# In-projection of a two-layer diffusion step: more unused products at the start, adaLN units turned one chunk sooner, the last quarter's weights in the load list

## The chip, the core and the metric

The kernel runs on one core of a Trainium2 chip. The core has a matrix engine (TensorE, PE, whose loads of the stationary operand are listed apart as PEld), VectorE (DVE), ScalarE (ACT), GpSimd (POOL), and SyncE (SP), which here issues every DMA. Each engine executes its own instructions in the order in which the program holds them and waits on semaphores for the others. The metric is the device time of one launch, in microseconds; the median of three runs before the change is 2295.28 us.

## What is computed

One inference step of a transformer with two layers, on 128 context tokens and 128 latent tokens. Both groups use the same weights; the latent tokens also attend to cached keys. Only the first sub-layer matters for this case:

```python
mod = silu(cond) @ w_ada[l] + b_ada[l]                 # shift, scale, gate of each sub-layer
sh1, sc1, gt1, sh2, sc2, gt2 = split(mod, 6)
h = rmsnorm(x, g_norm_mix[l]) * (1 + sc1) + sh1        # (256 tokens, 2048)
proj = h @ w_in                                        # 2048 -> 768 + 512 + 64 + 1024 + 256 + 256
q_lat, ckv, k_rope, qb, kb, vb = split(proj)
qa  = rmsnorm(q_lat, g_q) @ w_q_up
ckv = rmsnorm(ckv, g_kv)                               # latents of this call
ckv_all = concat([cached_ckv, ckv])                    # cached latents ahead of them
kv = ckv_all @ w_kv_up
kb = rope(rmsnorm(kb, g_kn))
```

Everything is float32. A product of two float32 matrices is made of three products of a format with fewer bits: each operand is split into a high part (a cast) and a low part (what the cast left over), and high x high, high x low and low x high are added up.

## The kernel before

**Layout.** Features lie on the 128 partitions, the 256 tokens of both groups side by side in the free dimension. `hx` holds the modulated rows: 16 tiles of 128 features, each with a high half and a low half. `w_in_ab` comes as blocks of 128 x 128; an output chunk of 128 features needs 16 of them.

**Stages of the in-projection.** The rows need adaLN scales and shifts that are themselves products with 2 MB to 4 MB of weights, so the projection doesn't wait for all of them. It goes over 23 output chunks several times, each time with a part of the 16 feature tiles, and adds to the result in SBUF: `part(whole, 0, 2, ...)` uses feature tiles 0 and 1, `part(halves, 2, 2, ...)` tiles 2 and 3, and `part(rest, 4 * q, 4, ...)` for q = 1, 2 and 3 four tiles each. The text calls the last three quarters 1, 2 and 3; quarter 3 is the last quarter. In a quarter a chunk is four blocks, three products each, so 12 products.

**AdaLN units.** A unit is 512 columns of the adaLN weights. Between chunks, `pair` multiplies the condition with two tiles of such weights (PE, tile `ada`), ACT copies the result (`am`), PE transposes it (L113), DVE reduces it and adds the bias (L455, L457), and the rows of the next quarter can be made from it (`rows`, that is `modulate`): per row two scalings, one on DVE (L688) and one on ACT (L691), a cast on ACT (L692) and a subtraction (L674). The table in `quarter(q)` says after which chunk each step comes. In quarters 1 and 2 the transposes and rows came after chunk 16, and `normed` (DVE) after chunk 12.

**Weights.** `feed` is a list written out by hand: tiles of adaLN weights and tiles of `w_in_ab` (16 blocks, 1 MB, tile `raw`, three buffers) in the order in which SP loads them, each as soon as a buffer of its kind is free. `lead(W, n)` runs before each chunk while a loaded tile of the list is left: it casts 8 blocks (two casts of four blocks on ACT, `wh`, L258, and two subtractions on DVE, `wl`, L259, both in `split`) until 12 blocks are ready. These casts are pinned in program order by `keep_order`. A tile that isn't in the list is loaded and cast inside `chunk()`, 8 blocks at a time, and a scheduler puts these where it thinks best. Before the change the list had 13 of the 18 tiles of `rest`; the last five, all of the last quarter, were outside.

**Beside the last quarter.** `finish(c)` starts the norms and ropes of queries, latents and keys as their chunks arrive. `deep` runs sums of further adaLN rows on DVE (L538, a custom op, two per loaded `block`), pinned, and `row_step` those on PE. `caches()` loads the cached latents (`ckc`) and keys and splits `ckc` into `kv_in`.

**The start.** PE first runs `WARM` products on zeros (L110, `acc<-am`), then the two first half units: sums of the scale unit, statistics of x, `spread` (the norm's factor over the partitions), transposes, sums of the shift unit, transposes, and then the first products with weights.

```python
def lead(W, n):
    while len(W.blocks) < n and (W.half or W.begun):
        W.ahead(keep_order)
```

Of the kernel before, what the change touches and what calls it, by code (L numbers as in the profile page):

```python
# [18 lines left out]
P = 128  # L19
D = 2048  # L20
KD = D // P
T = 128
# [27 lines left out]
    _n += _w  # L50
NCONST = _n
NEARLY = _AT["bada"][0] + 2 * KD
WARM = 9
RATE = {"in0": 0.35, "in": 0.5, "in3": 0.25, "heads": 0.72, "out0": 0.62, "c": 0.36, "outc": 0.36}
FRATE = {"up": 0.7, "down": 1.42}
PEW = {"heads": 1.0, "out0": 1.0, "c": 1.0}
# [38 lines left out]
def step_kernel(ctx: ExitStack, tc: tile.TileContext, A: dict):  # L95
# [24 lines left out]
    pe = TensorE()  # L120
# [44 lines left out]
    x = T_(keep, [P, KD, NT], "x")  # L165
# [69 lines left out]
    def acc_bank(n=None):  # L235
        if n is None:
            n = accs[turn["acc"] % len(accs)]
            turn["acc"] += 1
        return T_(pacc, [P, 512], f"acc{n}")
# [17 lines left out]
    def split(out_hi, out_lo, src, pin=lambda i: i):  # L257
        pin(act.copy(out_hi, src))  # L258
        pin(dve.tensor_tensor(out=out_lo, in0=src, in1=out_hi.bitcast(F32), op=ALU.subtract))  # L259
# [693 lines left out]
    def mixer_ab(hx, beside):  # L953
        l = 0
        with tc.tile_pool(name="ab", bufs=1) as ab:
            with tc.tile_pool(name="abp", bufs=1) as pj:
                T_(ab, [P, SHIFT // 4], "pad")
                spare = {"s3": T_(ab, [P, 4, 512], "kv_in")}
                ckc = T_(pj, [P, 4, T], "ckc")
# [3 lines left out]

                def caches():
                    keep_order(sp.dma_start(out=ckc, in_=A["cache_ckv"]))
                    split(kv_in[:, :, 0, T:2 * T], kv_in[:, :, 1, T:2 * T], ckc)
                    keep_order(sp.dma_start(out=kr[:, T:2 * T], in_=A["cache_krope"]))
                    keep_order(sp.dma_start(out=kg[:, :, T:2 * T], in_=A["cache_gqa_k"]))
                    keep_order(sp.dma_start(out=vg[:, 1], in_=A["cache_gqa_v"]))
# [35 lines left out]
                def half_sums(unit):  # L1005
                    pair_sums(("half", unit.j, unit.h), unit.sums)
# [6 lines left out]
                rest = Weights(A["w_in_ab"][6:], 4, 4, cycle=23)  # L1013
# [3 lines left out]
                def weights(w, parts=1):  # L1017
                    feed.add("raw", lambda: w.begin(parts))
# [20 lines left out]
                for q in (1, 2):  # L1039
                    for u, t in ((2 * q + 2, 0), (2 * q + 2, 2), (2 * q + 3, 0), (2 * q + 3, 2)):  # L1040
                        weights(rest)
                        units(u, t)
                        if (q, u, t) == (1, 4, 2):
                            feed.add("late", late_constants)
                    weights(rest)
                    weights(rest)
                feed.go()

                pe.in_turn = True
# [9 lines left out]
                for g in range(2):  # L1059
                    for i in range(4):  # L1060
                        pe.matmul(ps[:, g:g + 1], squared[:, i, g * T:(g + 1) * T], inv(D),
                                  start=(i == 0), stop=(i == 3))
# [7 lines left out]
                nts = scaled_rows(rb0, 0, 2)  # L1070
                unit = HalfUnit(0, 0, att_bank, att_bank)
                half_sums(unit)

                def first_rows():
                    unit.copy()
                    unit.turn()
                    for c in range(2):
                        begin_row(hx, nts[c], c)

# [71 lines left out]
                    yield  # L1151

                def finish(c):
                    if c == 7:
                        deep.silu()
                        deep.rate = SIDE["in3"]
                    if c < 6:
                        start(queries(c))
                    elif c < 10:
                        start(latents(c - 6))  # L1160
                    elif c == 10:
                        start(key_rope())
                    elif c < 13:
                        start(keys(c - 11))
                    elif c == 14:
                        start(values(0))
                    elif c == 15:
                        start(values(1))
# [22 lines left out]
                def normed(q):  # L1191
                    second["nt"] = []
                    for c in range(4 * q, 4 * q + 4):
                        h = T_(tmp, [P, NT], "nt", bufs=4)
                        keep_order(dve.tensor_tensor(out=h, in0=x[:, c], in1=rb0, op=ALU.mult))
                        second["nt"].append(h)
# [20 lines left out]
                def pair(u, t):  # L1217
                    unit_pair(ROWS[u], t)
                    if t == 2:
                        second["finish"] = ada_finish(*ROWS[u])  # L1220
                        second["finish"].pop(0)()

                def turned(q=0):
                    second["finish"].pop(0)()
                    if q:
                        rows(q)
# [14 lines left out]
                def quarter(q):  # L1241
                    u = 2 * q + 2
                    return {3: lambda: pair(u, 0), 6: lambda: pair(u, 2), 8: turned, 11: lambda: pair(u + 1, 0),
                            12: lambda: normed(q + 1), 14: lambda: pair(u + 1, 2), 16: lambda: turned(q + 1)}

                def at(steps):
                    return lambda c: steps[c]() if c in steps else None
# [7 lines left out]
                kv_in = T_(ab, [P, 4, 2, 3 * T], "kv_in", F32R)  # L1255
# [392 lines left out]
    with banks("pab") as ppool["ada"]:  # L1648
# [3 lines left out]
        ps = acc_bank()  # L1652
        for _ in range(WARM):
            keep_order(pe.matmul(ps, idle[:, :P], idle, start=True, stop=True))
# [5 lines left out]
        with tc.tile_pool(name="beside", bufs=1) as beside:  # L1660
            o = mixer_ab(hx, beside)
            with tc.tile_pool(name="raw", bufs=1) as rp:
                T_(rp, [P, SHIFT // 4], "pad")
                u = raw_tile(rp, "u")
# [5 lines left out]
    u = ffn(hx, W, *begun, 0, st)  # L1670
    stage[0] = "c"
    with tc.tile_pool(name="cc", bufs=1) as cp, banks("pc") as ppool["ada"]:
# [8 lines left out]
        u = mixer_c(cp, hx, W, begun[0], st)  # L1681
# [155 lines left out]
```

## Time and profile before

| | us |
|---|---|
| median of 3 runs (2294.23 to 2295.8) | 2295.28 |
| the profiled execution | 2295.23 |
| its span, first to last instruction | 2293.4 |
| PE busy | 2272.2 |
| DVE busy | 1880.7 |
| ACT busy | 1215.1 |
| mean granted clock of PE | 0.996 |

The profiled execution is 1.83 us longer than its span. How the lines are read: a row of the timeline has its start and length in us, the engine, the source line, the operation, the tile written and the tiles read, shapes and a count; in square brackets stands how long the engine was idle before it and what ended that. A row of a stretch has its bounds, then PE, PEld, DVE, ACT and POOL busy with their instruction counts, the granted clock of PE as a share of full speed, the share of the DMA engines and GB/s. A row of a group has busy time and mean length in ns, then idle time before the group. Products run into each other, so lengths overlap; distances of starts don't.

### The profile page before, as it was taken

To read this page: it belongs to the slowest core of one execution; us is meant where nothing else is said; L and a number is where in the kernel's file an instruction comes from. 1 tells how busy PE (TensorE), PEld (TensorE's weight loads), DVE (VectorE), ACT (ScalarE), POOL (GpSimd) and SP (SyncE) were. 2 spreads that over 40 slices of the span, in tenths; PEclk is the share of its full clock that TensorE was granted. 3 is DMA by queue.
4 is the path that set the end of the run, shared out by engine and by line. 5 is a ranking of instruction groups with operands and counts; after the bars stand their busy time and mean duration, and the time that the engine had idled before them with its cause. 6 is when DMAs were issued, how large, how long until landed. Compare 5 with 4: busy or idle time off the path is not lost.

```text
span 2293.4 us, 47509 instructions
## 1 busy us (share of the span) xinstructions
PE 2272.2 (99%) x19496; PEld 2180.4 (95%) x19496; DVE 1880.7 (82%) x2963; ACT 1215.1 (53%) x2049; POOL 190.9 (8%) x219
## 2 busy tenths in 40 slices
PE   9999999999999999999999999999999999999998
PEld 6788888999999999999999999999999999999998
DVE  4768878889989999999978988898899955666654
ACT  4446666765553355555575454557555434555543
POOL 0011104400000000001130000023000000000011
PEclk9999999999999999999999999999999999999999
DMA  9888988777778777777778888776677655555553
GB/s 394 363 354 307 333 329 349 288 264 255 260 259 296 293 274 258 257 268 257 286 292 301 324 316 308 264 273 224 255 260 258 256 201 196 191 198 189 200 188 127
DMA packets 100121, 617.14 MB, mean 269 GB/s; under 512 B 10752, under 2 KB 18880, under 8 KB 33344
## 3 DMA queue, kind: packets, MB, share of 16 engines
q1 hardware_dynamic: 99904, 614.11, 72.4%
q8 instruction: 153, 2.51, 0.4%
q14 instruction: 64, 0.52, 0.1%
HBM read 609.32 MB, written 4.75 MB: 268 GB/s over the span
## 4 chain that ended last, share of the span: by engine, by line
PE 96%; DVE 1%; DMA 1%; ACT 1%; POOL 1%; issue 0%; SPq 0%; DVEq 0%; ACTq 0%
PE acc L110 89%; PE ada L110 3%; PE att L110 2%; DMA raw<-w_in_ab 1%; PE misc L110 0%; DVE wl L259 0%; DMA araw<-w_ada 0%; PE att L113 0%; POOL dev L837 0%; PE ada L113 0%; PE misc L113 0%; ACT wh L258 0%; DVE x L1694 0%; POOL hxc L841 0%; DVE qb L1184 0%
## 5 line engine op out<-in xcount | busy, mean ns | idle before, releaser
L110 PE MATMUL acc<-hx,wh 128*128 128x256 f32 (+1 forms) x7232 | 1248.5, 278 | 3.7 <-ACT wh L258 1.5
L258 ACT CAST wh<-raw 128x1024 fp32r<-128x1024 f32 (+1 forms) x866 | 798.6, 938 | 825.5 <-PE acc L110 697.2
L259 DVE TENSOR_TENSOR wl<-raw,wh 128x1024 fp32r<-128x1024 f32 (+1 forms) x866 | 930.3, 1091 | 245.6 <-ACT wh L258 237.9
L110 PEld LDWEIGHTS acc<-hx,wh 128*128 128x128 f32 x7232 | 1092.8, 188 | 24.7 <-issue 14.2
L110 PE MATMUL acc<-hx,wl 128*128 128x256 f32 (+1 forms) x3616 | 1001.5, 277 | 0.8 <-DVE wl L259 0.7
L110 PEld LDWEIGHTS acc<-hx,wl 128*128 128x128 f32 x3616 | 680.0, 188 | 4.3 <-issue 1.7
L110 PE MATMUL acc<-g,wh 128*128 128x256 f32 x2816 | 478.8, 276 | 0.0
L110 PEld LDWEIGHTS acc<-g,wh 128*128 128x128 f32 x2816 | 423.9, 188 | 0.0
L110 PE MATMUL acc<-g,wl 128*128 128x256 f32 x1408 | 388.0, 276 | 0.0
L483 DVE CUSTOM_DVE_ANT_0 junk<-araw,condb 128x2048 f32<-128x2048 f32 x128 | 294.1, 2297 | 0.0
L110 PEld LDWEIGHTS acc<-g,wl 128*128 128x128 f32 x1408 | 264.2, 188 | 0.0
L211 POOL TENSOR_TENSOR sqacc<-sqacc,sq 128x256 f32<-128x256 f32 x62 | 72.2, 1165 | 1442.3 <-ACT sq L207 1437.6
L110 PE MATMUL acc<-hxc,wh 128*128 128x256 f32 (+1 forms) x1056 | 189.1, 281 | 0.0
L110 PEld LDWEIGHTS acc<-hxc,wh 128*128 128x128 f32 x1056 | 161.9, 188 | 1.8 <-issue 1.7
L110 PE MATMUL acc<-hxc,wl 128*128 128x256 f32 (+1 forms) x528 | 146.8, 278 | 0.0
L110 PEld LDWEIGHTS acc<-hxc,wl 128*128 128x128 f32 x528 | 99.5, 188 | 0.2
L110 PE MATMUL acc<-wh,hxc 128*128 128x256 f32 (+1 forms) x512 | 95.0, 283 | 0.8 <-DVE nt L848 0.8
L1587 ACT ACTIVATE cv<-acc,convw 128x256 f32<-128x256 f32 x169 | 94.4, 559 | 0.0
L538 DVE CUSTOM_DVE_ANT_0 hx<-block,condb 128x1024 fp32r<-128x1024 f32 x66 | 80.4, 1218 | 4.7 <-DMA block<-w_ada 4.4
L1593 DVE SCALAR_TENSOR_TENSOR cv<-acc,convw,cv 128x254 f32<-128x254 f32 x169 | 80.8, 478 | 3.2
L110 PEld LDWEIGHTS acc<-wh,hxc 128*128 128x128 f32 x512 | 79.4, 188 | 3.7 <-issue 2.5
L1590 DVE SCALAR_TENSOR_TENSOR cv<-acc,convw,cv 128x254 f32<-128x254 f32 x169 | 80.2, 474 | 0.0
(290 smaller groups left out, 1809.3 us busy)
## 6 DMA issues: line engine op xcount, KB each, us to landing
raw<-w_up SPq DMA_DIRECT2D x176, 1024.0 KB, 4.8
araw<-w_ada SPq DMA_DIRECT2D x132, 1024.0 KB, 6.2
raw<-w_down SPq DMA_DIRECT2D x88, 1024.0 KB, 4.8
raw<-w_in_c SPq DMA_DIRECT2D x48, 1024.0 KB, 6.9
block<-w_ada SPq DMA_DIRECT2D x42, 512.0 KB, 6.5
raw<-w_in_ab SPq DMA_DIRECT2D x18, 1024.0 KB, 9.0
raw<-w_out_ab SPq DMA_DIRECT2D x16, 1024.0 KB, 7.8
raw<-w_out_c SPq DMA_DIRECT2D x16, 1024.0 KB, 5.6
```

What stands on the lines that cost most here:

```text
L110: return self.placed(nc.tensor.matmul(*a, **kw))
L211: eng.tensor_tensor(out=st["acc"], in0=st["acc"], in1=sq, op=ALU.add)
L258: pin(act.copy(out_hi, src))
L259: pin(dve.tensor_tensor(out=out_lo, in0=src, in1=out_hi.bitcast(F32), op=ALU.subtract))
L483: keep_order(dve.tensor_tensor_reduce(out=T_(feat["pool"], [P, D], "junk"), in1=feat["row"][:, c], in0=feat["raw"].rearrange("p g n -> p ( ...
L538: keep_order(dve.tensor_tensor_reduce(out=self.junk, in0=self.raw, in1=self.row[:, c].rearrange("p (g n) -> p g n", g=2), scale=1.0, scala ...
L1587: pin(act.activation(y, ps, AF.Identity, scale=cw[:, 1, m:m + 1], bias=cw[:, 3, m:m + 1]))
L1590: pin(dve.scalar_tensor_tensor(out=y3[:, :, 1:], in0=p3[:, :, :T - 1], scalar=cw[:, 0, m:m + 1], in1=y3[:, :, 1:], op0=ALU.mult, op1=ALU.add))
L1593: pin(dve.scalar_tensor_tensor(out=y3[:, :, :T - 1], in0=p3[:, :, 1:], scalar=cw[:, 2, m:m + 1], in1=y3[:, :, :T - 1], op0=ALU.mult, op1=A ...
```

## The change

Five edits, all in the in-projection. `WARM` goes from 9 to 15. Four unused products (512 columns of x, into a bank that is overwritten later) are added: two behind the sums of the shift's half unit, two behind its transposes. In quarters 1 and 2 the second unit is turned, and the next quarter's rows are made, after chunk 15 and not after chunk 16. The split of the cached latents goes from `caches()` to chunk 3 of the last quarter. The five last tiles of `rest` are put into the list, so `lead` casts them as well.

```diff
-WARM = 9
+WARM = 15
...
                 def caches():
                     keep_order(sp.dma_start(out=ckc, in_=A["cache_ckv"]))
-                    split(kv_in[:, :, 0, T:2 * T], kv_in[:, :, 1, T:2 * T], ckc)
...
                     weights(rest)
+                    weights(rest)
+                for _ in range(5):
                     weights(rest)
                 feed.go()
...
                 half_sums(unit)
+                unused = acc_bank()
+
+                def idle_products(n):
+                    for _ in range(n):
+                        pe.matmul(unused, x[:, 0, :P], x[:, 0:2].rearrange("p c n -> p (c n)"), start=True, stop=True)
+
+                idle_products(2)
 
                 def first_rows():
                     unit.copy()
                     unit.turn()
+                    idle_products(2)
...
                 def finish(c):
+                    if c == 3:
+                        split(kv_in[:, :, 0, T:2 * T], kv_in[:, :, 1, T:2 * T], ckc)
...
-                            12: lambda: normed(q + 1), 14: lambda: pair(u + 1, 2), 16: lambda: turned(q + 1)}
+                            12: lambda: normed(q + 1), 14: lambda: pair(u + 1, 2), 15: lambda: turned(q + 1)}
```

**ACT in quarter 1, around the rows of quarter 2.** Before, from the cast ahead of the unit's copy; `wh` is a high half of weights, `am` the unit's copy, `nt` and `hx` the rows, `raw` a loaded tile:

```order
L258 CAST wh_1168<-raw_959 128x512 x2
L447 COPY am_1196<-ada_1115 128x512
L258 CAST wh_1212<-raw_959 128x512 x2
L691 ACTIVATE nt_1146<-nt_1146,mod_77,scl_78 128x128
L692 CAST hx_104<-nt_1146 128x256
L691 ACTIVATE nt_1148<-nt_1148,mod_77,scl_78 128x128
L692 CAST hx_104<-nt_1148 128x256
L691 ACTIVATE nt_1150<-nt_1150,mod_77,scl_78 128x128
L692 CAST hx_104<-nt_1150 128x256
L691 ACTIVATE nt_1152<-nt_1152,mod_77,scl_78 128x128
L692 CAST hx_104<-nt_1152 128x256
L258 CAST wh_1275<-raw_1043 128x512 x2
```

The same place of the changed program:

```order
L258 CAST wh_1179<-raw_970 128x512 x2
L447 COPY am_1207<-ada_1126 128x512
L691 ACTIVATE nt_1157<-nt_1157,mod_77,scl_78 128x128
L692 CAST hx_110<-nt_1157 128x256
L691 ACTIVATE nt_1159<-nt_1159,mod_77,scl_78 128x128
L692 CAST hx_110<-nt_1159 128x256
L691 ACTIVATE nt_1161<-nt_1161,mod_77,scl_78 128x128
L692 CAST hx_110<-nt_1161 128x256
L691 ACTIVATE nt_1163<-nt_1163,mod_77,scl_78 128x128
L692 CAST hx_110<-nt_1163 128x256
L258 CAST wh_1246<-raw_970 128x512 x2
L258 CAST wh_1286<-raw_1054 128x512 x2
```

The cast of chunks 18 and 19 (`wh_1212` before, `wh_1246` now) stood ahead of the rows and stands behind them.

**DVE in the last quarter, from the casts of chunks 14 and 15.** In the changed program; `proj` holds the latents, `kv_in` their split, `hx,mod<-block` are the deep sums, `kvb` and `kg` the keys, and `wl_2277` is the low half of the weights of chunks 16 and 17:

```order
L259 TENSOR_TENSOR wl_2197<-raw_1881,wh_2196 128x512 x2
L1120 SCALAR_TENSOR_TENSOR proj_130<-proj_130,cst_74,misc_2218 128x256 x4
L538 ISA hx_110,mod_77<-block_2102,condb_1873 128x1024
...
L259 TENSOR_TENSOR kv_in_1867<-proj_130,kv_in_1867 128x128 x5
L1195 TENSOR_TENSOR qb_252<-qb_252,acc_375_2313 128x256
...
L219 TENSOR_SCALAR rv_2245<-misc_2242 128x2
L538 ISA hx_110,mod_77<-block_2102,condb_1873 128x1024
...
L1145 SCALAR_TENSOR_TENSOR kvb_253<-kvb_253,cst_74,misc_2266 128x256
L896 TENSOR_TENSOR rope_2271<-kvb_253,cst_74 64x128 x2
L898 TENSOR_TENSOR kg_124<-kvb_253,cst_74 128x128
L899 TENSOR_TENSOR kg_124<-kg_124,rope_2271 128x128
L259 TENSOR_TENSOR wl_2277<-raw_1984,wh_2276 128x512
```

Before, the casts of the last quarter's end stood ahead of the latents' scaling (`wl_2394`, `wl_2398`), and both sums of the first block further ahead still:

```order
L538 ISA hx_104,mod_77<-block_2077,condb_1860 128x1024
...
L1184 TENSOR_TENSOR kvb_242<-kvb_242,acc_363_2225 128x256
L259 TENSOR_TENSOR wl_2394<-raw_2391,wh_2393 128x1024
L1184 TENSOR_TENSOR kvb_242<-kvb_242,acc_366_2249 128x256
L219 TENSOR_SCALAR rv_2161<-misc_2158 128x2
L1184 TENSOR_TENSOR qb_241<-qb_241,acc_370_2280 128x256
L259 TENSOR_TENSOR wl_2398<-raw_2391,wh_2397 128x512
L1184 TENSOR_TENSOR qb_241<-qb_241,acc_377_2310 128x256
L1111 SCALAR_TENSOR_TENSOR proj_124<-proj_124,cst_74,misc_2191 128x256 x4
L259 TENSOR_TENSOR kv_in_1852<-proj_124,kv_in_1852 128x128 x6
```

The casts of weights moved behind the latents and the first key, and the deep sums moved in between them.

**PE at the same place**, in the changed program, between the last products of chunk 15 (`acc_375`) and the first of chunk 16 (`acc_379`):

```order
L110 MATMUL acc_375_2313<-hx_110,wl_2197 128x256
L110 MATMUL misc_2242<-cst_74,sq_2216 128x1 x2
L113 MATMUL att_376_2327<-cst_74,kvb_253 128x128 x2
L110 MATMUL misc_2266<-cst_74,rr_2194 128x128 x2
L110 MATMUL misc_2301<-cst_74,rr_2247 128x128 x2
L110 MATMUL att_432_2627<-kg_124,qb_252 128x128
L110 MATMUL acc_379_2339<-hx_110,wh_2276 128x256 x2
L110 MATMUL acc_382_2366<-hx_110,wh_2276 128x256 x2
L110 MATMUL acc_379_2339<-hx_110,wl_2277 128x256
```

Five short products stand together ahead of chunk 16: statistics and factors of the keys, a transpose of values and the first scores. Each needs a result of DVE from the list above, and the factors share one bank of PSUM. Before, such products stood apart, between products of chunks.

## The prediction

> **What bounds the kernel.** First the page, then what TensorE waits for, then its timeline.
>
> ```profile
> span 2293.4 us, 47509 instructions
> PE 2272.2 (99%) x19496; PEld 2180.4 (95%) x19496; DVE 1880.7 (82%) x2963; ACT 1215.1 (53%) x2049; POOL 190.9 (8%) x219
> ```
>
> TensorE (PE) is idle for 2293.4 - 2272.2 = 21.2 us of the whole span. A change that leaves its work alone can therefore gain only out of these 21 us, and out of stretches with a lower clock; it can lose without limit, because every wait it adds to PE is added to the end. From the waits of PE between 25 and 340 us:
>
> ```profile
> PE acc L110 <- ACT wh L258: 1.5, 3, 0.8
> ```
>
> and, of stretches of 20 us, the one behind the in-projection (us, then PE, weight load, DVE, ACT, POOL, clock, DMA share, GB/s):
>
> ```profile
> 200.00:220.00 20.00, 20.00 (x159) 17.53 (x158) 18.61 (x50) 10.79 (x22) 2.81 (x4) 1.00 0.85 293
> ```
>
> In the stage that is edited PE waits three times for a cast of weights, 1.5 us in all, and behind it PE is full while VectorE (DVE) is busy for 18.6 of 20 us. So no later wait is there that could pay back what is lost here, and DVE has little room.
>
> **The start.** PE's timeline (start, length, idle before it) and its weight loads:
>
> ```profile
> 1.44 9.81 PE L110 MATMUL acc<-am 128*128 128x512 f32 x18 [1.44 <-DVE am L1651]
> ...
> 9.37 0.19 PEld L110 LDWEIGHTS acc<-am 128*128 128x128 f32 x1 [0.24 <-issue]
> 9.80 0.19 PEld L110 LDWEIGHTS acc<-am 128*128 128x128 f32 x1 [0.24 <-issue]
> ...
> 13.39 1.07 PE L110 MATMUL ada<-araw,condw 128*32 128x256 f32 x16 [2.14 <-DMA araw<-w_ada]
> ...
> 17.02 1.93 PE L110 MATMUL ada<-araw,condw 128*32 128x256 f32 x16
> ...
> 20.46 1.90 PE L110 MATMUL att<-ql,condw 128*32 128x256 f32 x16
> 22.17 1.06 PE L110 MATMUL att<-kv_in,condw 128*32 128x256 f32 x16
> 23.79 0.44 PE L113 MATMUL att<-cst,am 128*128 128x128 f32 x2 [0.56 <-ACT am L413]
> 25.41 0.97 PE L110 MATMUL acc<-hx,wh 128*128 128x256 f32 x2 [1.19 <-ACT hx L715]
> ```
>
> and the granted clock (seventh figure) in four of its microseconds:
>
> ```profile
> 15.00:16.00 1.00, 1.00 (x8) 1.00 (x8) 0.00 (x0) 0.00 (x0) 0.00 (x0) 0.69 1.03 434
> 22.00:23.00 1.00, 1.00 (x20) 0.38 (x12) 0.96 (x4) 0.62 (x1) 0.00 (x0) 0.90 1.03 430
> 25.00:26.00 1.00, 0.59 (x2) 0.39 (x3) 0.90 (x4) 1.00 (x5) 0.00 (x0) 0.81 1.02 411
> 29.00:30.00 1.00, 1.00 (x10) 1.00 (x10) 0.00 (x0) 0.37 (x1) 0.00 (x0) 0.99 1.04 434
> ```
>
> A mean of 0.69 between full and half means that the clock fell at 15.38; likewise it rose at 22.2, fell at 25.62 and rose at 29.02. The steps are 6.82, 3.42 and 3.40 us: decisions come every 3.41 us. The same sixteen sums take 1.93 at half clock and 1.07 at full.
>
> Each unused product is two passes of 9.80 - 9.37 = 0.43 us, so six more run from 11.25 to 16.41, while the first weights have been there since 13.39: 3.02 us later. The four new ones take 1.72 us a pair, where PE waited 0.56 and 1.19: 1.16 + 0.53 = 1.69 us more. If the clock then stays up, this comes back: 0.86 on the second sums, 0.84 on the third, half of 3.41 = 1.70 on the first products of weights. Of the 5.1 us at half clock between 15.38 and 20.46, the second sums are 1.93; of the 3.2 left at most half would go, and part is GpSimd's power, so I take 1.3. That is 4.7 against 3.02 + 1.69 = 4.71: **nothing**. Nor would a gain last:
>
> ```profile
> 52.58 13.85 DMA raw<-w_in_ab
> ...
> 74.03 0.47 PE L110 MATMUL acc<-hx,wh 128*128 128x256 f32 x2 [0.17 <-DVE qb L1184]
> ```
>
> The first row is from the chain of work, the second from PE: a load of weights that lands at 66.43 sets the work up to 74.03, and PE already waits 0.17 there. So the low end of this term is 0; the high end, where the new products don't hold the clock at the decisions near 18.8 and 22.2, is 0.84 + 1.70 = +2.5. I take 0.
>
> **Units turned one chunk sooner.** A chunk is four blocks of weights, 12 products. Quarter 1, PE and then ScalarE (ACT):
>
> ```profile
> 107.47 0.60 PE L113 MATMUL ada<-cst,am 128*128 128x128 f32 x4
> ...
> 109.30 0.39 PE L110 MATMUL acc<-hx,wh 128*128 128x256 f32 x2
> ...
> 110.66 0.39 PE L110 MATMUL acc<-hx,wh 128*128 128x256 f32 x2
> ...
> 112.61 0.51 PE L110 MATMUL acc<-hx,wh 128*128 128x256 f32 x2 [0.43 <-ACT wh L258]
> 113.46 0.38 PE L110 MATMUL acc<-hx,wl 128*128 128x256 f32 x1 [0.34 <-DVE wl L259]
> ```
>
> ```profile
> 108.60 0.49 ACT L691 ACTIVATE nt<-nt,mod,scl 128x128 f32<-128x128 f32 x1 [2.16 <-DVE mod L457]
> ...
> 111.95 3.74 ACT L258 CAST wh<-raw 128x512 fp32r<-128x512 f32 x7
> ```
>
> A chunk takes 110.66 - 109.30 = 1.36 us. The transposes start at 107.47, ACT makes the rows from 108.60, and only behind them come casts, from 111.95. PE can go on with them at 112.61, 5.14 us after the transposes; three chunks of ready weights cover 4.71 of that, and PE waits 0.43 and 0.34.
>
> The order of ACT in the changed program shows what the earlier turn does: the cast that stood ahead of the rows (for chunks 18 and 19) now stands behind them. The rows move ahead by a chunk, but the first cast behind them is needed two chunks sooner. Only two chunks lie between transposes and that cast, 4.71 - 1.36 = 3.35 us, against the same 5.14: PE waits 1.79 and 0.34, **1.36 more**. All eight ACT instructions of the rows and the DVE ones beside them move along, so nothing gets shorter. Behind the waiting product stand all later products of the quarter; DVE's adds of those chunks wait for PE, and with the later cast SP gets its buffer of weights later, which costs nothing as long as the 8 blocks ahead last. Quarter 2 has the same steps:
>
> ```profile
> 149.85 0.60 PE L113 MATMUL ada<-cst,am 128*128 128x128 f32 x4
> ...
> 155.37 0.50 PE L110 MATMUL acc<-hx,wh 128*128 128x256 f32 x2 [0.82 <-ACT wh L258]
> 156.21 0.39 PE L110 MATMUL acc<-hx,wl 128*128 128x256 f32 x1 [0.34 <-DVE wl L259]
> ...
> 152.22 0.60 ACT L258 CAST kv_in<-ckc 128x512 fp32r<-128x512 f32 x1
> ```
>
> Here the split of the cached latents stood between the rows, some 0.5 us of ACT with its overlap; it goes to the last quarter, where ACT is free before the first result. So 1.36 - 0.5 = +0.9. Together **+2.3**. Ends: -1.93 if ACT kept its lead and the present waits of 0.77 and 1.16 went; +5.7 if the clock also fell behind both waits (1.7 each).
>
> **The last quarter.** Its weights now come through the list, so their casts are pinned in program order with the pinned sums of the adaLN rows (the custom op). Between the casts of chunk 14 and the first low half that chunk 16 needs (wl_2277), DVE's order now holds four scalings, eight latent splits, two adds and both sums of a block, all behind a product that itself waits for chunk 13. Their prices, DVE from 160 to 212 us (busy, mean ns):
>
> ```profile
> L538 DVE CUSTOM_DVE_ANT_0 hx<-block,condb 128x1024 fp32r<-128x1024 f32 x4 | 4.9, 1218 | 0.1
> L1184 DVE TENSOR_TENSOR qb<-qb,acc 128x256 f32<-128x256 f32 x10 | 4.1, 417 | 1.5 <-PE acc L110 1.3
> L259 DVE TENSOR_TENSOR wl<-raw,wh 128x512 fp32r<-128x512 f32 x4 | 2.8, 688 | 0.2
> L259 DVE TENSOR_TENSOR kv_in<-proj,kv_in 128x128 fp32r<-128x128 f32 x8 | 1.9, 284 | 0.3 <-ACT kv_in L258 0.3
> L1111 DVE SCALAR_TENSOR_TENSOR proj<-proj,cst,misc 128x256 f32<-128x256 f32 x4 | 1.7, 474 | 1.3 <-PE misc L110 1.3
> L896 DVE TENSOR_TENSOR rope<-kvb,cst 64x128 f32<-64x128 f32 x4 | 1.1, 287 | 0.1
> L1136 DVE SCALAR_TENSOR_TENSOR kvb<-kvb,cst,misc 128x256 f32<-128x256 f32 x2 | 1.0, 476 | 0.5 <-PE misc L110 0.5
> L219 DVE TENSOR_SCALAR rv<-misc 128x2 f32<-128x2 f32 x5 | 0.8, 150 | 0.0
> ```
>
> Two low halves 1.38, four scalings 1.7, two sums 2.44, eight splits 1.9, two adds 0.83, one scaling 0.48, four rope steps at 0.29 each 1.15 and a statistic 0.15 make 10.0 us; neighbours overlap a little (four scalings take 1.7, not 1.9), so I take 9.0. PE has 20 products of chunks 14 and 15 (1.36 / 12 each, 2.3), four of the next pair (0.45) and small ones, about 1.5 by the short rows above: 4.3. PE waits **4.7** (up to 5.7; 0 if DVE were ahead, which the product behind chunk 13 speaks against). A wait of that kind covers most of a clock window, and at 25.62 waits of 0.56 and 1.19 were enough; half clock for 3.41 us costs 1.7, less what PE waits anyway: **+1.0** (0 to 1.7). Casts in halves: 2 x 0.69 for 1.3 a pair by ACT's and DVE's rows, hidden by the lead of 8 blocks, **+0.3** (0 to 1.5). On SP the four loads of caches and that of the condition now stand behind two more tiles of weights, and the next stage's weights behind outputs that wait for latents and keys. The cached latents have to land before chunk 0 ends, the others before PE leaves the quarter; by their places both do, so 0, and up to 1 where one is late. The deep sums' blocks move too, but their DVE time is in the 9.0.
>
> [...]
>
> **Sum.** The profiled execution took 2295.23, 1.83 more than its span and 0.05 under the median of 2295.28. 2295.23 + 0 + 2.3 + 4.7 + 1.0 + 0.3 = **2303.5**.
>
> **Rivals.**
> [...]
> - The pile is hidden, because DVE gets to the sums early: 2295.23 + 2.3 + 0.3 = 2297.8. For: DVE idles before. Against: the order. 0.17.
> - The clock falls behind the rows' waits too, and the start isn't held: 2303.5 + 2 x 1.7 + 1.2 = 2308. 0.13.
> - Not slower: the casts keep their lead. Place: the first chunk whose weights are cast behind the rows, or behind the pile. If that cast is done within 3.35 us of the transposes, PE never waits, and 0.77 + 1.16 go: 2293.3. For: DVE and ACT have idle time. Against: 5.14 measured. It also covers that the edits do what they say. 0.10.
>
> **How the numbers follow.** The forecast has 0.45. The first three cases and it lie on 2297.8 to 2308; 2296.5 to 2308.5 takes in their unknown terms and leaves out the last one and little above. 0.2% (4.6 us) is about what a measurement can tell here: slower is 0.45 + 0.15 + 0.13 = 0.73, the pile hidden and most of the last case are the same, 0.24, faster 0.03.
>
> **What would show it.** Quarters 1 and 2: waits of PE for the cast behind the rows of 1.8 us each, one chunk earlier than now. Last quarter: PE waits ahead of chunk 16 for DVE, 4 to 5 us with small pieces, and a granted clock of 0.5 behind it. Start: first products of weights near 27, at full clock, and the wait at 74 gone or as now. Wrong would be no wait over 1 us between 100 and 210.

## The result, and the profile after

| | median us | runs from, to |
|---|---|---|
| before | 2295.28 | 2294.23 to 2295.8 |
| changed | 2305.46 | 2303.78 to 2305.89 |

The ratio is 1.004, its 95% interval 1.0029 to 1.0051. The forecast was 2303.5, the range 2296.5 to 2308.5. First the page of the changed kernel, then the kinds of wait of TensorE (PE) whose longest is over 0.7 us and which are new or longer in sum (us in total, times, longest):

```profile
span 2303.7 us, 47568 instructions
PE 2279.2 (99%) x19516; PEld 2182.6 (95%) x19516; DVE 1881.2 (82%) x2972; ACT 1215.8 (53%) x2058; POOL 188.6 (8%) x219
```

```profile
PE acc L110 <- ACT wh L258: 4.4, 3, 1.7
PE acc L110 <- ACT kn L1366: 2.0, 1, 2.0
PE misc L110 <- POOL rr L222: 1.9, 2, 1.0
PE misc L110 <- DVE rv L219: 1.5, 1, 1.5
...
PE att L113 <- DVE kvb L1195: 0.8, 1, 0.8
```

The span is 10.3 us longer, but PE's idle time grew only from 21.2 to 24.5: the unused products fill idle time at the start and count as busy, and behind two waits the same products ran at half clock (0.50 for 3.41 us each).

**Where the time went.** Each of these programs has 18,072 products with weights (`wh` or `wl`). The start of the n-th of them in one trace less that in the trace of before says how late a kernel is at that place. The table gives it at the places where before stood at 104 us and so on, worked out from the traces, together with each kernel's measured median less that of before on the same chip. Between 175 and 230 us the products of adaLN rows stand in another order in some kernels, which shifts the difference by about 2 us either way, so the table goes by 260. The same happens at some later places: by the columns that the products without weights move, an estimate, split_alone and cast_ahead look about 4 us earlier at 300 than they are, changed, start_alone and no_turn about 2 us earlier at 330, and list_alone about 2 us later at 260.

| kernel | 104 | 120 | 165 | 260 | 300 | 330 | 360 | 2290 | medians |
|---|---|---|---|---|---|---|---|---|---|
| changed | -0.2 | 0.9 | 2.2 | 6.8 | 6.8 | 8.1 | 11.3 | 10.2 | +10.2 |
| start_alone | 0.5 | 0.5 | 0.5 | 1.0 | 1.0 | -1.8 | 2.7 | 1.6 | +1.0 |
| turn_alone | -1.0 | 2.0 | 4.6 | 2.6 | 2.6 | 2.4 | 11.2 | 10.5 | +10.6 |
| list_alone | -0.9 | -0.9 | 3.2 | 10.8 | 9.1 | 9.7 | 15.9 | 15.3 | +14.7 |
| split_alone | -0.3 | -0.5 | -0.2 | -1.1 | -3.5 | -2.2 | -0.6 | 0.6 | +0.8 |
| no_list | 0.2 | 3.0 | 4.5 | 3.9 | 3.0 | 3.4 | 13.6 | 12.9 | +14.5 |
| no_turn | -0.1 | -0.3 | -0.7 | 4.0 | 4.0 | 3.8 | 7.0 | 6.2 | +5.9 |
| cast_ahead | -0.2 | -1.7 | -3.5 | -0.3 | -2.7 | -1.4 | 0.1 | 1.6 | +1.7 |
| turn_cast_ahead | 0.1 | -0.1 | 0.0 | 0.0 | 0.0 | 0.0 | 0.0 | 0.0 | +0.6 |
| cast_ahead_q1 | -1.2 | -2.7 | -2.7 | -2.3 | -2.3 | -2.3 | -2.3 | -2.2 | -2.1 |
| no_turn_sums_late | 1.0 | 0.8 | 0.4 | 8.1 | 8.0 | 8.0 | 8.1 | 13.5 | +13.1 |
| turn_fewer_sums | -1.1 | -0.1 | 2.5 | 0.7 | 0.7 | 0.5 | 0.2 | 11.5 | +12.9 |
| cast_ahead_14 | -0.2 | -1.7 | -1.6 | -2.0 | -2.0 | -2.0 | -2.0 | 0.8 | -1.1 |

The changed kernel loses 2.4 us between 104 and 165 (the rows), 4.6 between 165 and 260 (the last quarter) and 3.4 to 4.5 between 300 and 360 (the stage behind). Three views show the places.

The start and the rows of quarters 1 and 2, PE (start, length, idle before it):

```profile
26.33 0.78 PE L110 MATMUL acc<-hx,wh 128*128 128x256 f32 x2
...
105.95 0.60 PE L113 MATMUL ada<-cst,am 128*128 128x128 f32 x4
...
111.02 0.50 PE L110 MATMUL acc<-hx,wh 128*128 128x256 f32 x2 [1.72 <-ACT wh L258]
111.85 0.38 PE L110 MATMUL acc<-hx,wl 128*128 128x256 f32 x1 [0.33 <-DVE wl L259]
...
149.84 0.60 PE L113 MATMUL ada<-cst,am 128*128 128x128 f32 x4
...
154.90 0.50 PE L110 MATMUL acc<-hx,wh 128*128 128x256 f32 x2 [1.72 <-ACT wh L258]
```

and ScalarE (ACT) at the first of them:

```profile
107.01 0.49 ACT L691 ACTIVATE nt<-nt,mod,scl 128x128 f32<-128x128 f32 x1 [1.78 <-DVE mod L457]
...
110.35 3.22 ACT L258 CAST wh<-raw 128x512 fp32r<-128x512 f32 x6
```

From the transposes to the first product with the cast behind the rows it is 111.02 - 105.95 = 5.07 us (5.14 before). That did not change; only the work that covers it did, three chunks before and two now.

The last quarter, PE and then VectorE (DVE):

```profile
193.10 0.44 PE L113 MATMUL att<-cst,kvb 128*128 128x128 f32 x2 [0.76 <-DVE kvb L1195]
195.01 0.68 PE L110 MATMUL misc<-cst,rr 128*128 128x128 f32 x4 [1.47 <-DVE rv L219]
196.60 1.22 PE L110 MATMUL misc<-cst,rr 128*128 128x128 f32 x4 [0.91 <-POOL rr L222]
...
197.90 1.20 PE L110 MATMUL acc<-hx,wh 128*128 128x256 f32 x4
```

```profile
188.52 1.29 DVE L259 TENSOR_TENSOR wl<-raw,wh 128x512 fp32r<-128x512 f32 x2
...
191.29 1.22 DVE L538 CUSTOM_DVE_ANT_0 hx<-block,condb 128x1024 fp32r<-128x1024 f32 x1
...
194.71 0.15 DVE L219 TENSOR_SCALAR rv<-misc 128x2 f32<-128x2 f32 x1
194.78 1.22 DVE L538 CUSTOM_DVE_ANT_0 hx<-block,condb 128x1024 fp32r<-128x1024 f32 x1
...
197.57 0.68 DVE L259 TENSOR_TENSOR wl<-raw,wh 128x512 fp32r<-128x512 f32 x1
```

DVE's pile runs from 188.52 to 198.25. PE waits in it three times, 3.14 us, for the add of a chunk of values (`kvb` holds keys and values), for a statistic of keys and for GpSimd's factor that follows from one; when the products of chunk 16 start, at 197.90, they wait for nothing more.

The stage behind, ACT, and then PE:

```profile
315.16 1.14 ACT L258 CAST wh<-raw 128x512 fp32r<-128x512 f32 x2 [1.33 <-DMA raw<-w_out_ab]
316.32 1.28 ACT L912 ACT_TABLE_LOAD   x1
...
318.61 0.47 ACT L1366 COPY kn<-acc 128x384 f32<-128x384 f32 x1
```

```profile
319.13 0.58 PE L110 MATMUL acc<-wh,kv_in 128*128 128x256 f32 x1 [2.02 <-ACT kn L1366]
```

and PE at the same place before:

```profile
311.21 0.38 PE L110 MATMUL acc<-wh,kv_in 128*128 128x256 f32 x1 [0.77 <-ACT kn L1355]
```

In the changed kernel ACT waits 1.33 us for a tile of the next stage's weights and then loads a table, and behind both stands the copy of the keys for which PE waits: 2.02 us, 0.77 before. The table load stood there before, too (at 308.40, 1.28 us as well); the cast with its wait is new in this place.

**The clock.** Pairs of stretches of 3.41 us, one behind the other (the first figure behind the comma is PE's busy time, the seventh the clock). Before:

```profile
22.20:25.61 3.41, 1.66 (x23) 0.74 (x15) 2.05 (x8) 1.77 (x6) 0.00 (x0) 1.00 1.02 418
25.61:29.03 3.42, 3.42 (x16) 3.23 (x16) 2.62 (x6) 2.52 (x7) 0.00 (x0) 0.50 1.02 424
```

The changed kernel:

```profile
151.71:155.13 3.42, 1.70 (x14) 1.50 (x14) 2.61 (x7) 3.32 (x9) 1.46 (x2) 1.00 0.79 331
155.13:158.54 3.41, 3.08 (x26) 2.87 (x26) 2.69 (x5) 2.96 (x7) 0.01 (x1) 1.00 0.34 77
192.68:196.09 3.41, 1.12 (x6) 0.72 (x6) 3.41 (x14) 1.36 (x4) 1.15 (x1) 1.00 0.74 239
196.09:199.50 3.41, 2.90 (x13) 2.90 (x14) 3.31 (x9) 2.58 (x6) 0.45 (x1) 0.50 0.49 169
315.55:318.97 3.42, 1.56 (x12) 1.24 (x10) 3.21 (x9) 3.39 (x9) 0.00 (x0) 1.00 0.81 322
318.97:322.38 3.41, 3.25 (x15) 2.63 (x19) 3.33 (x9) 2.17 (x7) 0.93 (x2) 0.50 0.39 138
```

The clock fell to 0.50 behind the pile and behind the keys, each time for 3.41 us, and held at 1.00 behind the rows, where PE had been idle for 1.72 of 3.42 us.

### The profile page after: what moved, and what is told of

It is laid out like the page before. It is cut to its first block, busy times and chain, and to the rows that moved or that the text cites. A ratio compares the mean times of both kernels' runs of the same rounds, so it can differ in the third digit from the quotient of the medians.

```text
span 2303.7 us, 47568 instructions
## 1 busy us (share of the span) xinstructions
PE 2279.2 (99%) x19516; PEld 2182.6 (95%) x19516; DVE 1881.2 (82%) x2972; ACT 1215.8 (53%) x2058; POOL 188.6 (8%) x219
## 4 chain that ended last, share of the span: by engine, by line
PE 96%; DMA 2%; DVE 1%; ACT 1%; issue 0%; POOL 0%; SPq 0%; DVEq 0%; ACTq 0%
PE acc L110 89%; PE ada L110 3%; PE att L110 2%; DMA kv_in<-w_ada 1%; DMA raw<-w_out_ab 1%; DMA araw<-w_ada 0%; PE misc L110 0%; PE att L113 0%; PE ada L113 0%; DVE wl L259 0%; DMA ckc<-cache_ckv 0%; PE misc L113 0%; DVE x L1705 0%; ACT wh L258 0%; ACT nt L691 0%
## 5 line engine op out<-in xcount | busy, mean ns | idle before, releaser
L110 PEld LDWEIGHTS acc<-hx,wh 128*128 128x128 f32 x7232 | 1091.8, 188 | 25.9 <-issue 11.2
## 6 DMA issues: line engine op xcount, KB each, us to landing
raw<-w_in_ab SPq DMA_DIRECT2D x18, 1024.0 KB, 10.5
```

What stands on the lines that cost most here:

```text
L110: return self.placed(nc.tensor.matmul(*a, **kw))
```

## The experiments

**Each edit alone.** Four kernels, each with one edit added to the kernel before (the diffs are the parts of the change shown above).

start_alone (`WARM = 15` and the four products):

> Only the unused products are added to the kernel before (15 for 9 at the start, and the four on x). Theory A (the start is paid back and no more): no fall of the granted clock between 10 and 36 us, first products of weights near 26.3, the transposes that stood at 60.56 some 0.2 to 0.3 earlier, the time 2295.0 within 0.7. Rival B (the gain of the start lasts): 0.8 to 1 us still gained at 120, 2294.3. Rival C (a shifted start alone changes what the scheduler makes of later stages, and the longer wait at the keys of the next stage comes from there): PE waits about 2 us for kn near 312 and the clock falls behind it, 2298.

2296.19 against 2295.15, ratio 1.0006 (0.9997 to 1.0015). The granted clock is 1.00 in every stretch from 8 to 360 us (0.998 over the whole execution, 0.996 before), and yet it is 0.5 late at 104: theory A in its place, and 1.2 us above its time, with an interval that still holds no change at all. Rival B is out, and so is C (PE waits 0.61 for `kn`, and the clock stays at 1.00 behind it). Its later differences (up to 2.7 at 360) come from stages that it doesn't touch; there PE waits 1.31 us for a low half of weights at 349.5.

turn_alone (`16: lambda: turned(q + 1)` becomes 15):

> Only the turn after chunk 15 in place of 16. Theory A (the first cast behind the rows is needed two chunks after the transposes): PE waits 1.7 and 0.3 in each quarter, 1.36 more in quarter 1 and 1.36 more in quarter 2, since there the split of the cached latents still stands between the rows (2.2 instead of 1.7): +2.5 to +3, 2298. Rival B (the waits are absorbed later, since SP and DVE set the pace behind them): waits as above but no more than +1 at the end, 2296. Rival C (the rows are finished earlier and later waits shrink): 2294.5.

2305.72, ratio 1.0044 (1.0031 to 1.0057): none of the three. By 165 it is 5.6 late against 104. PE's waits account for 2.6 of that (1.72, 2.1 and twice 0.34, less 1.93 before), the clock for most of the rest, since it fell behind both waits here (0.50 from 111.66 to 115.07 and from 156.03 to 159.44; half of each is 1.7, an estimate). The first of them:

```profile
108.24:111.66 3.42, 1.36 (x10) 0.96 (x9) 2.77 (x6) 3.36 (x9) 1.29 (x2) 1.00 0.00 0
111.66:115.07 3.41, 3.41 (x19) 3.41 (x18) 1.57 (x3) 1.63 (x4) 0.00 (x0) 0.50 0.68 228
```

The greater part comes at 345, in a stage that the edit doesn't touch. PE, ACT and DVE there:

```profile
351.29 0.80 PE L110 MATMUL acc<-hx,wh 128*128 128x256 f32 x2 [5.99 <-ACT hx L258]
```

```profile
350.87 0.37 ACT L258 CAST hx<-att 128x256 fp32r<-128x256 f32 x1 [11.60 <-DVE mod L538]
```

```profile
348.33 1.23 DVE L538 CUSTOM_DVE_ANT_0 hx<-block,condb 128x1024 fp32r<-128x1024 f32 x1 [2.32 <-DMA block<-w_ada]
```

The sums of the deep adaLN rows write their products, which nobody reads, into `hx`, into the place of the last heads (`deep.junk`). The cast of the last head has to wait for the last such sum (a second stands behind the one shown and ends at 350.83), the sums for their block.

list_alone (five more tiles in the list):

> Only the five last tiles of weights put into the list. Theory A (DVE's pile in the last quarter): PE waits 3 to 5 us ahead of chunk 16 of the last quarter, clock at half behind it, and up to 1 us for a cast at the quarter's first chunk; the next stage as before: +5 to +6, 2301. Rival B (the list also moves the next stage's loads, so the wait for kn of 2.0 us and the fall of the clock behind it come with it): 3 us more, +8 to +9, 2304. Rival C (without the split at chunk 3 the pile is hidden): +1, 2296.

2309.84, ratio 1.0061 (1.0048 to 1.0074). The pile is there, with waits of 0.75, 1.47 and 0.67, but also a wait of 2.39 for a cast at 164 and 5.1 us between 345 and 360. The wait for `kn` isn't. None of the three: the time is 5.8 us above rival B, the dearest, and PE doesn't wait at the place that rival B named.

split_alone:

> Only the split of the cached latents moved to chunk 3 of the last quarter. Theory A: it leaves the rows of quarter 2, so PE's waits of 0.82 and 0.34 there become 0.4 and 0.34; nothing else: 2294.8. Rival B (its four casts and subtractions now stand ahead of the casts of weights at the last quarter's first chunks, and PE waits up to 1 us there as in the changed kernel at 169): 2295.7. Rival C (the next stage's wait for kn of 2.0 us comes from here): 2298.

2295.95, ratio 1.0003 (0.9994 to 1.0012), no difference that can be told. No wait of the kind that rivals B and C named is there, and of theory A the shorter waits in quarter 2 did not come: from 150 to 160 PE is busy for 8.84 us, as before. The trace says why. The cast of the split on ACT still stands between the rows of quarter 2 (151.27 and 152.18 are rows):

```profile
151.67 0.61 ACT L258 CAST kv_in<-ckc 128x512 fp32r<-128x512 f32 x1
```

The split isn't pinned, so the scheduler puts it where it thinks best, and moving the call in the program did not move it.

The four differences add up to 27 us; all edits together cost 10.2. So the edits are not terms of one sum.

**One edit taken out of the changed kernel.**

no_list (the five tiles out again):

> The changed kernel without the five last tiles in the list (start, turn and split are in). Theory A (my terms): rows +2.3, start 0, no pile: PE waits of 1.72 and 0.34 near 110 and 154, 2297.5, and 1.7 more for each fall of the clock behind them. Rival B (the stages behind the quarter add a wait of their own in any changed order): 2 to 7 us more between 300 and 360, 2300 to 2305.

2310.06, ratio 1.006 (1.0048 to 1.0073): rival B in its place, and larger, 10.6 us between 300 and 360 where it had up to 7. Without the pile it is 14.5 us behind the kernel before, with it 10.2. 3.9 late at 260, it then waits 6.48 us for the last head's cast, as turn_alone did. In quarter 2 PE waits 2.11 us, as in turn_alone, and the split stands between the rows here too. And in quarter 1 the clock fell here, with PE as busy as in the changed kernel's stretch from 151.71 (1.70 us), behind which it held:

```profile
108.46:111.88 3.42, 1.70 (x13) 1.32 (x12) 2.77 (x7) 3.32 (x9) 1.47 (x2) 1.00 0.00 0
111.88:115.29 3.41, 3.08 (x15) 3.05 (x15) 2.53 (x5) 2.59 (x5) 0.00 (x0) 0.50 0.38 108
```

no_turn (turn after chunk 16 again):

> The changed kernel with the turn back after chunk 16 (start, list and split are in). Theory A: waits of 0.4 to 0.8 near 112 and 155 as before, the pile ahead of chunk 16 of the last quarter with about 3 us of waits and the clock behind it, +4.7 to +6 by 205, and 0 to 3 us more for the keys near 318: 2300 to 2304. Rival B (list without the earlier turn is worse, as list_alone, since the cast of chunk 0 of the last quarter waits 2.4 us): another 2 to 4 us by 165, 2306 to 2309.

2301.43, ratio 1.0029 (1.0017 to 1.004): theory A. The same three waits of 0.75, 1.47 and 0.91, and 1.95 for `kn` at 316. Behind the three DVE's next add of a chunk comes 4.85 us after the low half at 193.87; in the changed kernel, with 0.50 from 196.09 to 199.50, it comes 5.02 after the one at 197.57. At full clock it would be about 4.05 (an estimate: half of the 1.93 us from 197.57 to 199.50 less). So the clock fell here too, by that estimate, and neither the pile nor the wait for `kn` needs the turn. The pile belongs to the list (list_alone has it too); the wait for `kn` comes with the list beside the start or the split, which no run parts, since list_alone doesn't have it.

**The rows: is it the cast behind them?** An extra pair of casts ahead of the rows, once with the turn as before, once with the earlier turn:

```diff
                 def turned(q=0):
+                    if q:
+                        lead(rest, 16)
                     second["finish"].pop(0)()
```

> The kernel before with one call added: ahead of the transposes of quarters 1 and 2 (still after chunk 16) the casts are brought to 16 blocks, so one pair of casts more stands ahead of the rows on ScalarE. Theory A (the cast behind the rows sets the wait, and ScalarE's idle 2.16 us ahead of the rows holds the pair): PE's waits of 0.43 and 0.34 at 112 and of 0.82 and 0.34 at 155 vanish, 1.9 us gained by 165; the end 2293.4 if later stages keep it. Rival B (the rows' own chain sets it: the pair delays the rows and the next quarter's first chunk waits for hx): waits of 0.5 to 1 us move to 117 and 160, 2295. Rival C (later stages decide): gained by 165 as in A, given back between 190 and 360, 2295 to 2300.

> As turn_alone, with the casts brought to 16 blocks ahead of the transposes, so that the cast which the earlier turn pushed behind the rows stands ahead of them again. Theory A: the waits of 1.72 and 0.34 near 110 and 154 fall to 0.4 and 0.3 or less, no fall of the clock there, the offset at 165 under +0.5 against +4.6 of turn_alone. Rival B (the earlier transposes themselves cost it): waits stay above 1.2. The end is open by what comes behind 330, where turn_alone waited 6.0 us for a cast behind sums that waited for their block: 2294 if that comes from the shift of the rows, 2299 to 2301 if it stays.

cast_ahead: no wait of PE is left between 105 and 160, and from 104 to 165 it gains 3.3 us: theory A for the rows. It ends at 2297.23, ratio 1.0007 (0.9999 to 1.0016), since a cast outside the list came late in the last quarter, and behind that wait a pair of products took 0.63 us from 166.48 to 169.04 where it took 0.39 from 169.82 on. PE and ACT:

```profile
164.92 0.72 PE L110 MATMUL acc<-hx,wh 128*128 128x256 f32 x4 [2.60 <-ACT wh L258]
```

```profile
163.84 1.98 ACT L258 CAST wh<-raw 128x1024 fp32r<-128x1024 f32 x2
```

turn_cast_ahead: 2296.11, ratio 1.0001 (0.9992 to 1.001). The wait is back to 0.50, and from 120 to the end no place is more than 0.1 us off the kernel before:

```profile
112.79 0.50 PE L110 MATMUL acc<-hx,wh 128*128 128x256 f32 x2 [0.50 <-ACT wh L258]
```

This tells most. The earlier turn with the cast in its old place costs nothing and gains nothing; all 10.6 us of turn_alone, those at 345 too, follow from one pair of casts in each of the two quarters on the other side of eight instructions.

cast_ahead_q1, the extra pair in quarter 1 alone (`if q == 2:`):

> As cast_ahead, but the extra pair of casts stands ahead of the rows of quarter 1's turn alone. Theory A (the 2.6 us wait that cast_ahead had at 165 comes from the pair taken in quarter 2, which uses up the listed weights one pair sooner): no wait over 0.5 near 112, the one of 0.8 at 155 as before, none over 0.5 at 165, 0.8 to 1.4 gained by 165; the end 2294 if it is kept. Rival B (later stages decide): gained by 165, 2295.5 to 2297 at the end.

2293.55 against 2295.64, ratio 0.9993 (0.9984 to 1.0001), the fastest of all, with an interval that just holds no change. PE from 100 to 120 here, and before:

```profile
100.00:110.00 10.00, 10.00 (x87) 8.43 (x87) 7.09 (x19) 3.81 (x8) 0.00 (x0) 1.00 0.41 153
110.00:120.00 10.00, 10.00 (x90) 10.00 (x89) 8.45 (x19) 6.86 (x15) 1.60 (x2) 1.00 1.01 403
```

```profile
100.00:110.00 10.00, 10.00 (x88) 8.43 (x87) 6.93 (x19) 2.96 (x7) 0.00 (x0) 1.00 0.41 143
110.00:120.00 10.00, 9.23 (x77) 8.82 (x76) 8.24 (x17) 7.91 (x16) 1.48 (x2) 1.00 0.97 381
```

177 products instead of 165, 12 of 0.113 us each: two waits of 0.77 in sum were worth 1.4. Idle time tells less than what is lost: away from the waits a product of 0.28 us starts 0.11 after the one ahead of it, so at each of the two waits some 0.17 us count as busy in which no further product starts, and the products behind the waits are longer as well (0.51 for the first pair where 0.39 is usual, 0.38 for 0.28). ACT had room ahead of the rows:

```profile
104.08 2.18 ACT L258 CAST wh<-raw 128x512 fp32r<-128x512 f32 x4
108.82 0.49 ACT L691 ACTIVATE nt<-nt,mod,scl 128x128 f32<-128x128 f32 x1 [2.56 <-DVE mod L457]
```

Of its 2.2 us, 1.2 were there at 104 already, which the edit doesn't reach; about 1.4 come at the rows; 0.4 of the gain goes again between 165 and 260.

cast_ahead_14, the pair in both quarters and one tile more in the list:

> cast_ahead (an extra pair of casts ahead of the rows of both turns, still after chunk 16) with one more tile in the list, 14 instead of 13. Theory A (cast_ahead lost its gain at 165 because a cast outside the list came late on ScalarE there; one more listed tile lets the pinned casts go on): no wait over 0.8 near 112, 155 and 165, 3 us gained by 175, the end 2292 to 2293.5 if kept. Rival B (any listed tile of the last quarter pins casts ahead of the rows' other work and puts the wait elsewhere in that quarter): 1 to 4 us of waits between 165 and 205, 2295 to 2299. Rival C (the order of the later stages decides): the offset at 205 is kept as far as 300 and 2 to 10 us are lost behind it, 2297 to 2303.

2294.39 against 2295.46, ratio 0.9993 (0.9984 to 1.0003). 3.2 us are gained from 104 to 158, and then PE waits 1.25 for a cast at 160.88; it is 2.0 ahead from 260 to 1185. Between theory A and rival B. Rival C is out. (Its profiled execution lost 2.8 us behind 1185, which this study doesn't explain.)

**The pile and the sums.** no_turn with the deep sums begun later:

```diff
                     if c == 7:
                         deep.silu()
+                    if c == 16:
                         deep.rate = SIDE["in3"]
```

> As no_turn, but the sums on VectorE of the deep rows begin behind chunk 16 of the last quarter instead of chunk 7, so the two that stood in the pile (1.22 each) stand behind it; nothing is left out. Theory A (VectorE's pile sets the waits of 0.75, 1.47 and 0.91 ahead of chunk 16): they sum to 0.7 or less instead of 3.1, no fall of the clock, the offset to the kernel before at 205 is +1 to +2 instead of +5.5. Rival B (the waits come from the other rows, scalings, splits and key rows, or from GpSimd's factor): at least 2 us of them stay. The end: 1 us behind that at 205 if the later stages follow, 2297; more if the sums, begun later, hold up the last heads (3 to 6 us near 345).

Without the two sums in the pile, 2.44 us of DVE, PE's three waits of 3.13 become two of 1.91:

```profile
191.18 0.68 PE L110 MATMUL misc<-cst,rr 128*128 128x128 f32 x4 [1.24 <-DVE rv L219]
192.53 0.68 PE L110 MATMUL misc<-cst,rr 128*128 128x128 f32 x4 [0.67 <-DVE kvb L1146]
```

So the sums made 1.2 of the 3.1. The rest, 1.91, stays: nearer to rival B. Which of the other rows or GpSimd's factor makes it wasn't tried. The time is 2308.78, ratio 1.0055 (1.0042 to 1.0069). New waits of 1.43 and 1.22 us come behind the pile, the mean granted clock is 0.996 where no_turn has 0.998, and 5 us more go at 441, where PE waits for a shift that the late sums make.

turn_alone with `"heads": 1.6` for `"heads": 1.9` in `SIDE`, so fewer sums in the heads' stage:

> As turn_alone, with 1.6 in place of 1.9 steps of the deep rows' sums per pump in the stage of the heads, so fewer of them stand ahead of the last head's cast; the rest runs in the next stage, nothing is left out. Theory A (that cast stands behind sums that wait for their block, and this makes the 6.0 us): the wait near 345 falls under 2 us, the end at +3.5 to +6 (2299 to 2301), the waits of 1.72 and 2.1 near 110 and 154 stay. Rival B (the last head's own chain is late): 6 us stay, 2305.

The 6.0 us at 345 are gone (0.2 late at 360 against 11.2), so they were the sums: theory A for the place. But the end is at 2308.53, ratio 1.0058 (1.0045 to 1.007), since the sums left over hold up the first product of the next sub-layer, whose shift they make:

```profile
439.85 0.58 PE L110 MATMUL acc<-u,wh 128*128 128x258 f32 x1 [6.96 <-ACT u L752]
```

## Why the prediction was right, and where it was not

- **The start, 0:** inside its range, and probably some 0.8 too cheap. It is -0.2 at 104 in the changed kernel and +0.5 alone, where the medians differ by 1.0 and 0 isn't excluded. PE works from 1.44 to 26.33 nearly without a gap (0.03 us idle up to 30), at a granted clock of 1.00 wherever the profile shows one, and the first product of weights starts 0.9 later than before; most of that comes back from the half clock that is saved. But the payback of 4.7 was worked out from one trace, and that trace had 10.24 us at half clock ahead of 30 us, where of the other kernels with the old start turn_alone has 3.4, list_alone 6.8 and split_alone 10.3 (worked out from the mean clock of stretches of 2 us). At 104 the nine old starts lie between -1.2 and 0.1 (-0.5 in the mean), the five new ones between -0.2 and 1.0 (+0.3).
- **The rows, +2.3:** right, in size (2.4 by 165) and in place. The waits are 1.72 and 0.33 where 1.79 and 0.34 were forecast, one chunk earlier. turn_cast_ahead and cast_ahead show that the cast's place is the cause. The 0.5 taken off for the split came out as 0.4 (a wait of 1.72, in turn_alone 2.11), but for another reason than the prediction gave. Moving the split's call does nothing to its place: split_alone and no_list, which have it moved, still show it between the rows, with waits of 0.82 and 2.11. The list takes it away: in the changed kernel the load of the cached latents is issued at 159.97 (140.99 before), behind more tiles of weights, so they aren't there yet when the rows are made. In list_alone the split is gone from the rows with its call in the old place, and the wait of 0.82 is 0.45.
- **The pile, +4.7, its clock, +1.0, and the casts, +0.3:** the place is right and the sizes are off. DVE's rows took 9.7 us (9.0 forecast), but PE's waits are 3.14, since PE had 6.2 us to do from 188.52 to 197.90 and not the 4.3 that I had put down. The step behind that was wrong too: PE waits for the chunk of values, the statistic and the factor whose short products stand ahead of chunk 16, and the low half of its weights, on which the sum rested, is ready in time when they are done. The clock fell as forecast (0.50 from 196.09 to 199.50). The casts cost 0.98 + 0.17 - 0.21 = 0.9, three times the 0.3, at 169 and 173, where PE waits for `wh` and `wl`. Together 4.6 by 260, 6.0 forecast.
- **The split's new place and the caches, 0 up to 1:** "By their places both do, so 0" was wrong for the cached latents. They land at 165.79, when chunk 0 has been added (164.16), and ACT, which the prediction called free there, waits for them; the cast for which PE waits follows at 168.34:

```profile
165.79 0.62 ACT L258 CAST kv_in<-ckc 128x512 fp32r<-128x512 f32 x1 [6.22 <-DMA ckc<-cache_ckv]
```

```profile
169.01 1.03 PE L110 MATMUL acc<-hx,wh 128*128 128x256 f32 x4 [0.98 <-ACT wh L258]
```

In no_turn the split stands five instructions further back, at 163.66, waits for nothing, and PE has no such wait. That the late latents make the 0.98 is read from these rows; no run changes them alone. If it is so, most of the 0.9 above is this term's and not the casts'.
- **Behind the quarter, 0 up to 1:** this step failed. The changed kernel is 6.8 late at 300 and 10.0 at 315. The rows show that the next stage's weights land later against ACT's work (the second tile takes from 302.66 to 315.14, before from 292.69 to 300.23), and that PE waits 1.25 longer for the keys and then runs 3.41 us at a clock of 0.50. That the first makes the second is argued: ACT's wait of 1.33 is about what PE waits more, but no run takes it away alone. That the clock can fall a second time was in the rivals, but at the rows.
- So 2303.5 came near to 2305.46 by two errors of opposite sign: the last quarter 1.4 too dear, the stage behind 3 us too cheap. And it was luck that a third thing stayed away, of which the prediction says nothing: turn_alone and no_list lose 9 and 10 us between 330 and 360, where the last head's cast stands behind sums that wait for their block. The changed kernel and no_turn don't; why isn't known.
- **The rivals.** The 0.15 among the chances stood for a clock that holds behind the pile, 2302.5. No run shows that: it was 0.50 behind the pile from 196.09 to 199.50, and 0.50 from 196 to 200 in list_alone. The pile is hidden: no. The clock falls behind the rows: not in the changed kernel's profiled execution, but in turn_alone's (0.50 from 111.66 and from 156.03) and no_list's (0.50 from 111.88). "Not slower" was right in its condition, the cast ahead of the rows, which cast_ahead_q1 makes true with another edit.

## What to carry to other kernels

Ahead of a step that occupies an engine, count how many units of ready work the waiting engine has left until the first result queued behind the step; moving the step earlier was free here only where that result moved ahead of it as well (0.6 us in turn_cast_ahead, 10.6 in turn_alone). Take each edit of a bundle alone and out: here four edits cost 1.0, 10.6, 14.7 and 0.8 us singly and 10.2 together. A background stream (here the deep rows' sums) can turn an early delay into a later one (5.99 us at 345 in turn_alone), and putting it off moved the place where it is paid (6.96 us at 440 in turn_fewer_sums). And where a scheduler is free, look in the trace for where an instruction ended up before giving it a price: the split was moved in the program and stayed where it was, until a later load pushed it away.

## What the runs showed of the hardware

In the traces of before and of the changed kernel the granted clock is 1.00 or 0.50. Up to 2280 us it changed at 15.37, 22.20, 25.61 and 29.03 us before (6.83, 3.41 and 3.41 apart) and at 196.09, 199.50, 318.97 and 322.38 in the changed kernel (3.41, 119.47 and 3.41 apart, where 119.47 is 35 times 3.413). Cut into stretches of 3.41 us from these places, the two traces have six stretches at full clock, from 4 us on, in which PE is idle for more than 0.9 us. Behind 2.29 (from 192.68, changed), 1.86 (from 315.55, changed), 1.75 (from 22.20, before) and 1.43 (from 11.96, before) the clock was 0.50; behind 1.72 (from 151.71) and 1.45 (from 107.34), both in the changed kernel, it stayed at 1.00. Of the stretches above, it fell behind 2.06 and 2.11 in turn_alone (from 108.24 and 152.62) and behind 1.72 in no_list (from 108.46).

Idle time isn't all of it. In list_alone the clock fell at about 17.4 us (0.85 over 16 to 18, 0.50 over 18 to 20), and PE was busy for 3.97 of the 4 us from 14 to 18. PE ran sixteen products of one column there (14.24 to 16.19), but the changed kernel ran the same sixteen from 17.23 to 19.18 at 1.00, so that alone doesn't explain it. What decides isn't shown. A wait of 1.72 and 0.33 us cost about 2 us where the clock held (from 107.34, changed) and nearly 4 where it fell (an estimate: half of 3.41 us more). Whether this also makes executions of one kernel differ isn't shown, since each run has one trace; those of the changed kernel differ by 2.1 us, and those of the kernel before, which has no such wait, by up to 3.
